# Moving the conditioning products of a two-block transformer between stages, and summing each of their steps in SBUF

## The chip, the cores and the metric

The kernel runs on one core of one Trainium2 chip. The metric is the device time of one execution, in microseconds (us). A core has five engines with queues of their own, each of which issues in order: TensorE (PE; its weight loads are shown apart as PEld), VectorE (DVE), ScalarE (ACT), GpSimd (POOL) and SyncE (SP), which issues DMAs; POOL issues DMAs too. TensorE's clock is granted in two levels, 1.2 and 2.4 GHz; a profile shows the granted level as a share of the full one.

## The reference

Two transformer blocks follow each other on 256 tokens of width 1024, all in float32. The first has two layers (a mixer, a feed-forward of 4096, a gated side input). The second has two layers with a second stream, the context, and its normalisations are shifted, scaled and gated by six rows of 1024 that a conditioning vector gives. This is the part that the change moves:

```python
for i in range(DEPTH):
    mod = (s_lat @ w_mod[i] + b_mod[i])[:, None, :]
    mod_c = s_ctx @ w_mod[i] + b_mod[i]
    sh1, sc1, g1, sh2, sc2, g2 = jnp.split(mod, 6, axis=-1)
    sh1c, sc1c, g1c, sh2c, sc2c, g2c = jnp.split(mod_c, 6, axis=-1)
    h = rms_norm_2(x, norm_mix[i]) * (1.0 + sc1) + sh1
    hc = rms_norm_2(xc, norm_mix[i]) * (1.0 + sc1c) + sh1c
    ...
    x = x + g1 * y
    h = rms_norm_2(x, norm_ffn[i]) * (1.0 + sc2) + sh2
    x = x + g2 * swiglu(h, w_gate[i], w_up[i], w_down[i])
```

`w_mod` is 2 x 1024 x 6144 floats. The products `s @ w_mod` depend on no token, so they can be computed anywhere ahead of their first use. Below, modulation (l, j) is the row j of layer l: 0 sh1, 1 sc1, 2 g1, 3 sh2, 4 sc2, 5 g2.

## The kernel before, in words

The main chain is four layers one after another: `block1_layer` twice (a mixer, its output projection, a layer norm, a feed-forward of eight groups, a second layer norm, a gated addition) and `block2_layer` twice (a mixer, its output projection, a normalisation, a feed-forward of eleven groups). A projection with float32 accuracy is three passes over the halves of a split: `wh` and `wl` are high and low part of a weight tile (ACT makes `wh` on line 214, DVE `wl` on line 216, from a tile that SP has loaded four units ahead), `xh` and `xl` those of the data. Beside the main chain runs other work that needs no result of it: the context stream, and the 12 modulations.

A modulation is four items of `part` (line 940, L952 its load, L954 its matmuls, L962 its addition). An item takes two k-steps. A k-step loads 128 rows of `w_mod` (512 KB) through a DMA that POOL issues into one of two buffers named `fr` (the first six into `bc`), and multiplies them with the conditioning vectors in four matmuls, one for each quarter of 256 columns, each in 32 columns of the array of its own. So there are 48 items and 96 k-steps in all. The four items of a modulation add up in one PSUM tile `fil`, of which there is one buffer, held from the first item to the last; then DVE adds the bias row (line 962) and, save for the gates, a matmul on line 968 turns the row.

Where an item stands is written in lists. `program` is a list of (weights needed, function); `weave` spreads one list through another, `side_by_side` puts the items of a second list between the pieces of a feed-forward. In the first layer, modulations (0,0), (0,1) and (0,2) are woven into the mixer (`mix`), (0,3) beside the first feed-forward group (`first`), and (0,4) stands at the layer's end (`last`). In the second, (0,5) and (1,0) are in the mixer, (1,1) in `first`, (1,2) in `last`. In the third there is none. In the fourth, (1,3), (1,4) and (1,5) are woven into the second half of the mixer and into the output projection (`swa`). A scheduler then orders the instructions of each engine by its own estimate of times, within about the place that the lists give.

Other things that POOL does in the same queue matter here: line 385 computes the power of a half for every normalisation (`stb`, from `sta` of DVE).

Of the kernel before, what the change touches and what calls it, by code (L numbers as in the profile page):

```python
# [10 lines left out]
F32 = mybir.dt.float32  # L11
# [3 lines left out]
ALU = mybir.AluOpType  # L15
# [104 lines left out]
def body(ctx: ExitStack, tc: tile.TileContext, A: dict, out: bass.AP):  # L120
# [817 lines left out]
    def modulation(l, box, js):  # L938
# [3 lines left out]
        def part(j, u):  # L942
# [3 lines left out]
            if u == 0:  # L946
                st[j] = PT("fil")
            ps = st[j]
            for k in (2 * u, 2 * u + 1):
                early[0] += 1  # L950
                raw = T([P, D], F32, "bc" if early[0] <= 6 else "fr", 2)
                nc.gpsimd.dma_start(raw, A["w_mod_2"][l, k * P:(k + 1) * P, j * D:(j + 1) * D])  # L952
                for g in range(4):
                    mm(ps[32 * g:32 * g + 32, 0:256], cT[:, k, :], raw[:, 256 * g:256 * g + 256],  # L954
                       start=(k == 0), stop=(k == KD - 1), tile_position=(0, 32 * g))
            if u < 3:
                return
            bm = T([P, 256], F32, "gate" if j in (2, 5) else "bm", 3 if j in (2, 5) else 1)
            V.memset(bm, 0.0)
            for s in range(2):  # L960
                nc.gpsimd.dma_start(bm[s:P:32, :], A["b_mod_2"][l, j * D:(j + 1) * D].rearrange("(g n) -> g n", g=4))
            V.tensor_tensor(bm, ps[:, 0:256], bm, ALU.add)  # L962
# [452 lines left out]
    def block2_layer(l, xT, pr, box, ce, done, side):  # L1415
# [30 lines left out]
        if l == 1:  # L1446
            rest = dense[:16] + weave(dense[16:] + g, side["swa"][:8])
            att = attention(e, pr, l, range(6), ce, y)
            prog += weave(rest, att[:-1], True) + [do(rows)] + weave(att[-1:], outp[:1])
            prog += weave([do(gla_out, e, y)] + outp[1:], side["swa"][8:-2]) + side["swa"][-2:]  # L1450
# [208 lines left out]
    def mod(l, *js):  # L1659
        return modulation(l, boxes[l], js)  # L1660

    program += block1_layer(0, xTs[0], to_next(1), dict(tail=flat(ctx_a[:1]), lr=4, mix=mod(0, 0, 1) + ctx_n + mod(0, 2), first=flat(ctx_a[1:2]) + mod(0, 3), ffn=ctx_a[2:-2],
                                                        end=flat(ctx_a[-2:]), last=mod(0, 4)))
    program += block1_layer(1, xTs[1], to_next(2), dict(tail=[], lr=6, mix=mod(0, 5) + mod(1, 0), first=mod(1, 1), ffn=ctx_b[:-2],
                                                        end=flat(ctx_b[-2:]), last=mod(1, 2)))
# [6 lines left out]
        "na": ffn_n, "swa": ffn_c, "pre": [], "from": 2, "ffn": [do(layer2_params, 1, prs[1])] + G(["norm", "kv", "znv", "gla"]), "end": L(["nk", "skv"])})  # L1672
    program += block2_layer(1, xTs[3], prs[1], boxes[1], ce1, to_next(4), {
        "swa": mod(1, 3, 4, 5), "from": 11, "ffn": [], "end": [],
# [51 lines left out]
```

## Time and profile before

| | us |
|---|---|
| three runs | 1934.02, 1938.44, 1940.81 |
| median | 1938.44 |
| the profiled execution | 1940.12 |
| its span, first to last instruction | 1938.3 |
| PE busy in it | 1862.2 (96%) |
| DVE, ACT, POOL busy | 1217.7, 984.7, 117.1 |

A row of a timeline gives the start in us, the duration, the engine, the line, the operation, what it writes and reads, the count of merged instructions, and in brackets how long the engine was idle before it and what ended that. One k-step is x8 there (four matmuls of two passes each).

### The profile page before, as it was taken

How to read it: one execution, taken by the hardware profiler on the slowest of the kernel's cores; microseconds unless marked ns; L12 is line 12 of the kernel's file. 1: busy time of each engine (PE TensorE's matmuls, PEld its weight loads, DVE VectorE, ACT ScalarE, POOL GpSimd, SP SyncE). 2: the span in 40 equal slices, each digit the busy share in tenths (PEclk: the TensorE clock that was granted, in tenths of full speed). 3: DMA queues.
4: the chain of work that ended last, by engine and by line, in shares of the span. 5: the costliest groups of instructions: out<-in, count | busy, mean ns of one | idle time of the engine just before them, and what ended most of it. 6: DMA issues, size and time to landing. Idle time of an engine off the chain costs nothing. (4 is left out here: it accounts for less than half of the span.)

```text
span 1938.3 us, 31903 instructions
## 1 busy us (share of the span) xinstructions
PE 1862.2 (96%) x12481; PEld 1586.0 (82%) x12481; DVE 1217.7 (63%) x2317; ACT 984.7 (51%) x1622; POOL 117.1 (6%) x194
## 2 busy tenths in 40 slices
PE   8989999999999999999899999999999999879997
PEld 6756798897887698887687899899999986659997
DVE  5564656656666656667576776685646776655555
ACT  6453455544555455553557664454556655334443
POOL 3111100000110100000000000000000001100000
PEclk9998999999999999999899999999999999989999
DMA  8744754545666654556453445556555455346563
GB/s 295 247 161 152 231 187 153 185 153 190 212 218 203 210 165 137 168 176 204 147 169 94 133 151 170 183 170 192 181 185 164 144 168 180 110 152 184 183 179 107
DMA packets 101411, 338.84 MB, mean 175 GB/s; under 512 B 12148, under 2 KB 13388, under 8 KB 101260
## 3 DMA queue, kind: packets, MB, share of 16 engines
q1 hardware_dynamic: 86124, 286.00, 46.3%
q0 software_dynamic: 15136, 50.80, 7.8%
q8 instruction: 98, 1.61, 0.3%
q14 instruction: 53, 0.43, 0.1%
HBM read 335.70 MB, written 1.05 MB: 174 GB/s over the span
## 5 line engine op out<-in xcount | busy, mean ns | idle before, releaser
L216 DVE TENSOR_TENSOR wl<-wr,wh 128x1024 fp32r<-128x1024 f32 (+3 forms) x562 | 638.1, 1137 | 400.2 <-ACT wh L214 397.0
L214 ACT CAST wh<-wr 128x1024 fp32r<-128x1024 f32 (+3 forms) x562 | 549.6, 980 | 639.5 <-PE acc L281 145.5
L279 PE MATMUL acc<-wh,mh 128*128 128x256 f32 (+3 forms) x400 | 132.0, 335 | 0.3 <-ACT mh L357 0.2
L280 PE MATMUL acc<-wl,mh 128*128 128x256 f32 (+3 forms) x400 | 130.8, 328 | 0.5 <-DVE wl L216 0.5
L281 PE MATMUL acc<-wh,ml 128*128 128x256 f32 (+3 forms) x400 | 130.6, 329 | 0.0
L279 PE MATMUL acc<-wh,xh 128*128 128x512 f32 (+3 forms) x304 | 117.9, 398 | 2.8 <-ACT xh L378 1.9
L280 PE MATMUL acc<-wl,xh 128*128 128x512 f32 (+3 forms) x304 | 119.8, 395 | 0.5 <-DVE wl L216 0.5
L281 PE MATMUL acc<-wh,xl 128*128 128x512 f32 (+3 forms) x304 | 117.7, 388 | 0.1
L850 PE MATMUL acc<-wh,a 128*128 128x512 f32 x256 | 101.5, 400 | 0.0
L852 PE MATMUL acc<-wh,a 128*128 128x512 f32 x256 | 101.1, 396 | 0.0
L851 PE MATMUL acc<-wl,a 128*128 128x512 f32 x256 | 101.0, 395 | 0.0
L1470 PE MATMUL sc<-xh,wh 128*128 128x256 f32 x352 | 100.6, 286 | 0.0
L1471 PE MATMUL sc<-xl,wh 128*128 128x256 f32 x352 | 100.3, 285 | 0.0
L1472 PE MATMUL sc<-xh,wl 128*128 128x256 f32 x352 | 100.2, 285 | 0.0
L1471 PE MATMUL sc<-ml,wh 128*128 128x256 f32 x352 | 98.8, 281 | 0.0
L1472 PE MATMUL sc<-mh,wl 128*128 128x256 f32 x352 | 98.7, 280 | 0.0
L1470 PE MATMUL sc<-mh,wh 128*128 128x256 f32 x352 | 98.6, 280 | 0.0
L954 PE MATMUL fil<-fr,cT 128*32 128x256 f32 x720 | 67.2, 419 | 28.1 <-DMA fr<-in_w_mod_dram 27.8
L952 POOL DMA_DIRECT2D fr<-in_w_mod_dram x90 | 48.5, 541 | 709.8 <-PE fil L954 581.7
L279 PEld LDWEIGHTS acc<-wh,mh 128*128 128x128 f32 x400 | 74.9, 189 | 14.1 <-issue 4.7
L280 PEld LDWEIGHTS acc<-wl,mh 128*128 128x128 f32 x400 | 75.3, 188 | 7.7 <-DVE wl L216 1.4
L281 PEld LDWEIGHTS acc<-wh,ml 128*128 128x128 f32 x400 | 75.1, 188 | 6.4 <-issue 0.6
(574 smaller groups left out, 4780.7 us busy)
## 6 DMA issues: line engine op xcount, KB each, us to landing
wr<-in_ffn_w_dram SPq DMA_DIRECT2D x128, 512.0 KB, 3.4
fr<-in_w_mod_dram POOLq DMA_DIRECT2D x90, 512.0 KB, 5.1
wr<-in_w_gate_dram SPq DMA_DIRECT2D x66, 512.0 KB, 3.7
wr<-in_w_up_dram SPq DMA_DIRECT2D x66, 512.0 KB, 4.3
wr<-in_w_down_dram SPq DMA_DIRECT2D x66, 512.0 KB, 4.0
wr<-in_w_in_dram SPq DMA_DIRECT2D x40, 384.0 KB, 3.3
wr<-in_ev_w_in_dram SPq DMA_DIRECT2D x28, 512.0 KB, 4.9
wr<-in_w_in_dram SPq DMA_DIRECT2D x28, 512.0 KB, 4.2
```

What stands on the lines that cost most here:

```text
L214: S.copy(hi, raw)
L216: V.tensor_tensor(lo, raw, hi, ALU.subtract)
L279: mm(o, xh[:, k, :], wh[:, kk, :], start=(u == 0 and kk == 0), stop=False)
L280: mm(o, xh[:, k, :], wl[:, kk, :], start=False, stop=False)
L281: mm(o, xl[:, k, :], wh[:, kk, :], start=False, stop=(u == nu - 1 and kk == 1))
L850: mm(o, hh[:, b, ts_], wh[:, kk, :], start=(b == 0), stop=False)
L851: mm(o, hh[:, b, ts_], wl[:, kk, :], start=False, stop=False)
L852: mm(o, hl[:, b, ts_], wh[:, kk, :], start=False, stop=(b == 3))
L954: mm(ps[32 * g:32 * g + 32, 0:256], cT[:, k, :], raw[:, 256 * g:256 * g + 256], start=(k == 0), stop=(k == KD - 1), tile_position=(0, 32 * g))
L1470: mm(o, wh[:, kk, bs], mh, start=(k == 0 and b == 0), stop=False, skip_group_check=True)
L1471: mm(o, wh[:, kk, bs], ml, start=False, stop=False, skip_group_check=True)
L1472: mm(o, wl[:, kk, bs], mh, start=False, stop=(k == 7), skip_group_check=True)
```

## The change

It does three things. An item now sums only its own two k-steps in PSUM and adds them to the row in SBUF, which is allocated, cleared and loaded with the bias at the first item; `fil` is free again after each item. Modulations (0,2), (0,3), (0,4), (1,1), (1,2) and (1,5) are put into the side lists of the four feed-forwards: (0,2) and (0,3) into the first, (0,4) and (1,1) into the second, (1,2) into the third, (1,5) into the fourth. In the last layer the remaining two, (1,3) and (1,4), stand in the second half of the mixer, and its output projection has none beside it.

```diff
@@ -944,22 +944,21 @@
                 box["mf"] = T([P, 6, 2, KD], F32, "mf", 2)
             mf = box["mf"]
             if u == 0:
-                st[j] = PT("fil")
-            ps = st[j]
+                bm = st[j] = T([P, 256], F32, "gate" if j in (2, 5) else "bm", 3 if j in (2, 5) else 1)
+                V.memset(bm, 0.0)
+                for s in range(2):
+                    nc.gpsimd.dma_start(bm[s:P:32, :], A["b_mod_2"][l, j * D:(j + 1) * D].rearrange("(g n) -> g n", g=4))
+            bm, ps = st[j], PT("fil")
             for k in (2 * u, 2 * u + 1):
                 early[0] += 1
                 raw = T([P, D], F32, "bc" if early[0] <= 6 else "fr", 2)
                 nc.gpsimd.dma_start(raw, A["w_mod_2"][l, k * P:(k + 1) * P, j * D:(j + 1) * D])
                 for g in range(4):
                     mm(ps[32 * g:32 * g + 32, 0:256], cT[:, k, :], raw[:, 256 * g:256 * g + 256],
-                       start=(k == 0), stop=(k == KD - 1), tile_position=(0, 32 * g))
+                       start=(k == 2 * u), stop=(k == 2 * u + 1), tile_position=(0, 32 * g))
+            V.tensor_tensor(bm, ps[:, 0:256], bm, ALU.add)
             if u < 3:
                 return
-            bm = T([P, 256], F32, "gate" if j in (2, 5) else "bm", 3 if j in (2, 5) else 1)
-            V.memset(bm, 0.0)
-            for s in range(2):
-                nc.gpsimd.dma_start(bm[s:P:32, :], A["b_mod_2"][l, j * D:(j + 1) * D].rearrange("(g n) -> g n", g=4))
-            V.tensor_tensor(bm, ps[:, 0:256], bm, ALU.add)
             if j in (2, 5):
                 box[j] = bm
             else:
@@ -1444,10 +1443,10 @@
         outp = proj(("w_out_2", l), 8, HALVES, tiles_of(y), urgent(evac), (1,), first=l)
         g = gla(e, pr, lambda: ce.fin, True)
         if l == 1:
-            rest = dense[:16] + weave(dense[16:] + g, side["swa"][:8])
+            rest = dense[:16] + weave(dense[16:] + g, side["swa"])
             att = attention(e, pr, l, range(6), ce, y)
             prog += weave(rest, att[:-1], True) + [do(rows)] + weave(att[-1:], outp[:1])
-            prog += weave([do(gla_out, e, y)] + outp[1:], side["swa"][8:-2]) + side["swa"][-2:]
+            prog += [do(gla_out, e, y)] + outp[1:]
         else:
             main = weave(attention(e, pr, l, range(3, 6), ce, y), g) + [do(gla_out, e, y), do(rows)] + outp
             prog += weave(main, side["swa"][:-6]) + side["swa"][-6:]
@@ -1659,19 +1658,19 @@
     def mod(l, *js):
         return modulation(l, boxes[l], js)
 
-    program += block1_layer(0, xTs[0], to_next(1), dict(tail=flat(ctx_a[:1]), lr=4, mix=mod(0, 0, 1) + ctx_n + mod(0, 2), first=flat(ctx_a[1:2]) + mod(0, 3), ffn=ctx_a[2:-2],
-                                                        end=flat(ctx_a[-2:]), last=mod(0, 4)))
-    program += block1_layer(1, xTs[1], to_next(2), dict(tail=[], lr=6, mix=mod(0, 5) + mod(1, 0), first=mod(1, 1), ffn=ctx_b[:-2],
-                                                        end=flat(ctx_b[-2:]), last=mod(1, 2)))
+    program += block1_layer(0, xTs[0], to_next(1), dict(tail=flat(ctx_a[:1]), lr=4, mix=mod(0, 0, 1) + ctx_n, first=flat(ctx_a[1:2]),
+                                                        ffn=weave(ctx_a[2:-2], mod(0, 2, 3)), end=flat(ctx_a[-2:]), last=[]))
+    program += block1_layer(1, xTs[1], to_next(2), dict(tail=[], lr=6, mix=mod(0, 5) + mod(1, 0), first=[],
+                                                        ffn=weave(ctx_b[:-2], mod(0, 4) + mod(1, 1)), end=flat(ctx_b[-2:]), last=[]))
     ce1 = Stream(1)
     cl = ctx_last(ce1, prs[1], boxes[1])
     L = lambda ns: flat([cl[n] for n in ns])
     G = lambda ns: [it for n in ns for it in ([cl[n]] if n[0] != "g" and n != "norm" else cl[n])]
     ffn_n, ffn_c = ctx_ffn(boxes[0])
     program += block2_layer(0, xTs[2], prs[0], boxes[0], ce, to_next(3), {
-        "na": ffn_n, "swa": ffn_c, "pre": [], "from": 2, "ffn": [do(layer2_params, 1, prs[1])] + G(["norm", "kv", "znv", "gla"]), "end": L(["nk", "skv"])})
+        "na": ffn_n, "swa": ffn_c, "pre": [], "from": 2, "ffn": weave([do(layer2_params, 1, prs[1])] + G(["norm", "kv", "znv", "gla"]), mod(1, 2)), "end": L(["nk", "skv"])})
     program += block2_layer(1, xTs[3], prs[1], boxes[1], ce1, to_next(4), {
-        "swa": mod(1, 3, 4, 5), "from": 11, "ffn": [], "end": [],
+        "swa": mod(1, 3, 4), "from": 2, "ffn": mod(1, 5), "end": [],
         "pre": [do(lambda: last.update(fn=bcast_row(A["final_norm_2"])))]})
     run(program)
```

The queue of POOL around the layer norm in front of the first feed-forward, before: `stb` is the power for token tile 0 and then tile 1, `fr` the loads of k-steps (those of (0,3), then of (0,4)).

```order
L952 DMA fr_1987<-in_w_mod_dram 128x1024
L952 DMA fr_1993<-in_w_mod_dram 128x1024
L952 DMA fr_1999<-in_w_mod_dram 128x1024
L385 TENSOR_TENSOR stb_1672<-sta_1670,mhalf_67 128x1
L952 DMA fr_4649<-in_w_mod_dram 128x1024
L952 DMA fr_4655<-in_w_mod_dram 128x1024
L385 TENSOR_TENSOR stb_1723<-sta_1721,mhalf_67 128x1
```

The same place now (`h4stb` and `cstb` are powers of the mixer's head norm and of the context's norm):

```order
L385 TENSOR_TENSOR h4stb_1364<-h4sta_1362,mhalf_67 128x4
L385 TENSOR_TENSOR cstb_1386<-csta_1384,mhalf_67 128x1
L955 DMA fr_2333<-in_w_mod_dram 128x1024
L385 TENSOR_TENSOR stb_1630<-sta_1628,mhalf_67 128x1
L385 TENSOR_TENSOR stb_1681<-sta_1679,mhalf_67 128x1
L955 DMA fr_2442<-in_w_mod_dram 128x1024
L955 DMA fr_2448<-in_w_mod_dram 128x1024
```

No load stands between the two powers any more, and the loads of the feed-forward's first pairs stand around them.

TensorE at the end of the last layer's output projection, before: `L281` is the projection's last matmul, `L177` are the transposes of token tile 0 (`sc_17324`, `sc_17336`) and tile 1, `L1470` begins the feed-forward.

```order
L281 MATMUL acc_17348<-wh_17234,c_3068_15852 128x512
L954 MATMUL fil_17219<-fr_17410,cT_72 32x256 x4
L954 MATMUL fil_17219<-fr_17416,cT_72 32x256 x4
L954 MATMUL fil_17219<-fr_17422,cT_72 32x256 x4
L177 MATMUL sc_17324<-ident_61,a_3402_17321 128x128 x4
L177 MATMUL sc_17336<-ident_61,a_3402_17321 128x128 x4
L954 MATMUL fil_17219<-fr_17428,cT_72 32x256 x4
L954 MATMUL fil_17219<-fr_17434,cT_72 32x256 x4
L177 MATMUL sc_17386<-ident_61,a_3412_17383 128x128 x4
L177 MATMUL sc_17398<-ident_61,a_3412_17383 128x128 x4
L954 MATMUL fil_17219<-fr_17440,cT_72 32x256 x4
L985 MATMUL fil_19201<-gate_17446,cst_220 128x256 x2
```

And now, up to the feed-forward's first matmul (which is on line 1469):

```order
L957 MATMUL fil_17930<-fr_17937,cT_72 32x256 x4
L177 MATMUL sc_17377<-ident_61,a_3432_17374 128x128 x4
L957 MATMUL fil_18274<-fr_18275,cT_72 32x256
L177 MATMUL sc_17389<-ident_61,a_3432_17374 128x128 x4
L957 MATMUL fil_18274<-fr_18275,cT_72 32x256 x3
L957 MATMUL fil_18274<-fr_18281,cT_72 32x256 x4
L957 MATMUL fil_18618<-fr_18619,cT_72 32x256 x4
L177 MATMUL sc_17439<-ident_61,a_3442_17436 128x128 x4
L177 MATMUL sc_17451<-ident_61,a_3442_17436 128x128 x4
L957 MATMUL fil_18618<-fr_18625,cT_72 32x256 x4
L957 MATMUL fil_18962<-fr_18963,cT_72 32x256 x4
L1469 MATMUL sc_17469<-xh_17197,wh_17317 128x256
```

All but the last k-step of (1,5) stand ahead of the feed-forward, as before, although the list puts them into it. With two `fr` buffers, `fr_18275` can be loaded only after the pair ahead of it was used, `fr_18619` only after `fr_18275`, and `fr_18963` only after `fr_18619`.

TensorE in the first feed-forward before, between two weight tiles of an up part (`L825` to `L827` are its three passes):

```order
L825 MATMUL sc_2429<-xh_1607,wh_2384 128x256
L826 MATMUL sc_2429<-xl_1608,wh_2384 128x256
L827 MATMUL sc_2429<-xh_1607,wl_2386 128x256
L825 MATMUL sc_2428<-xh_1607,wh_2390 128x256
L826 MATMUL sc_2428<-xl_1608,wh_2390 128x256
L827 MATMUL sc_2428<-xh_1607,wl_2392 128x256
```

And in the same feed-forward now, where an item of (0,2) has been put:

```order
L825 MATMUL sc_2347<-xh_1565,wh_2284 128x256
L826 MATMUL sc_2347<-xl_1566,wh_2284 128x256
L827 MATMUL sc_2347<-xh_1565,wl_2286 128x256
L957 MATMUL fil_2441<-fr_2442,cT_72 32x256 x4
L957 MATMUL fil_2441<-fr_2448,cT_72 32x256 x4
L825 MATMUL sc_2346<-xh_1565,wh_2290 128x256
L826 MATMUL sc_2346<-xl_1566,wh_2290 128x256
```

In the feed-forwards the two k-steps of an item mostly stand together like this, with the next item some 100 to 350 matmuls further on. In the second layer's mixer, where (0,5) and (1,0) stand, the order of before is thinned out: 8 items where 16 were between the first layer's end and the second feed-forward.

## Rows read from the trace of the kernel before

**Rows 1.** The page: busy time by engine, and the granted clock in 40 slices.

```profile
PE 1862.2 (96%) x12481; PEld 1586.0 (82%) x12481; DVE 1217.7 (63%) x2317; ACT 984.7 (51%) x1622; POOL 117.1 (6%) x194
PEclk9998999999999999999899999999999999989999
```

**Rows 2.** Waits: who waited for whom, us in total, times, longest.

```profile
POOL fr L952 <- PE fil L954: 581.7, 56, 200.0
...
PE fil L954 <- DMA fr<-in_w_mod_dram: 27.8, 12, 7.4
```

**Rows 3.** Stretches: length, busy us and counts by engine, granted clock, DMA share, GB/s.

```profile
140.00:165.00 25.00, 19.16 (x112) 13.20 (x111) 7.48 (x27) 3.44 (x13) 2.11 (x4) 0.59 0.47 160
207.70:226.15 18.45, 15.93 (x82) 11.52 (x80) 14.22 (x24) 5.95 (x9) 3.44 (x7) 0.91 0.93 316
618.00:633.00 15.00, 11.00 (x53) 5.84 (x52) 5.01 (x26) 3.35 (x12) 1.85 (x4) 0.66 0.44 151
661.00:677.20 16.20, 12.27 (x66) 7.74 (x64) 14.85 (x32) 9.60 (x20) 6.21 (x9) 0.86 0.82 284
940.00:960.00 20.00, 12.20 (x61) 9.30 (x62) 9.48 (x22) 8.30 (x18) 1.93 (x4) 0.73 0.45 155
1715.50:1736.60 21.10, 9.92 (x70) 5.60 (x69) 9.91 (x22) 9.43 (x19) 3.60 (x6) 0.70 0.52 176
1400.00:1500.00 100.00, 100.00 (x664) 91.09 (x664) 53.92 (x66) 55.95 (x64) 0.00 (x0) 1.00 0.57 173
```

**Rows 4.** The page's groups: busy us, mean ns of one, idle before.

```profile
L954 PE MATMUL fil<-fr,cT 128*32 128x256 f32 x720 | 67.2, 419 | 28.1 <-DMA fr<-in_w_mod_dram 27.8
```

**Rows 5.** Timeline, TensorE, end of the first mixer.

```profile
145.22 1.08 PE L954 MATMUL fil<-fr,cT 128*32 128x256 f32 x8 [4.54 <-DMA fr<-in_w_mod_dram]
...
164.96 0.50 PE L279 MATMUL acc<-wh,mh 128*128 128x512 f32 x1
```

**Rows 6.** Timeline, layer norm in front of the first feed-forward.

```profile
214.40 0.15 DVE L383 TENSOR_SCALAR sta<-ag 128x1 f32<-128x1 f32 x1
218.39 0.53 POOL L952 DMA_DIRECT2D fr<-in_w_mod_dram  x1 [2.31 <-PE fil L954]
218.94 0.58 POOL L385 TENSOR_TENSOR stb<-sta,mhalf 128x1 f32<-128x1 f32 x1
226.15 0.28 PE L825 MATMUL sc<-xh,wh 128*128 128x256 f32 x1
```

**Rows 7.** Timeline, second layer: its attention, then the layer norm behind it.

```profile
622.41 1.08 PE L954 MATMUL fil<-fr,cT 128*32 128x256 f32 x8 [4.00 <-DMA fr<-in_w_mod_dram]
...
668.33 0.14 DVE L383 TENSOR_SCALAR sta<-ag 128x1 f32<-128x1 f32 x1
...
670.34 1.43 POOL L385 TENSOR_TENSOR stb<-sta,mhalf 128x1 f32<-128x1 f32 x1
```

**Rows 8.** Timeline, end of the second layer.

```profile
949.83 0.43 DVE L962 TENSOR_TENSOR gate<-fil,gate 128x256 f32<-128x256 f32 x1 [2.54 <-PE fil L954]
...
950.77 0.15 DVE L412 TENSOR_TENSOR ms<-ms 128x1 f32<-128x1 f32 x1
```

**Rows 9.** Timeline, end of the last output projection.

```profile
1715.50 1.07 PE L954 MATMUL fil<-fr,cT 128*32 128x256 f32 x16
1716.47 1.05 POOL L952 DMA_DIRECT2D fr<-in_w_mod_dram  x2 [13.52 <-PE fil L954]
1724.01 1.08 PE L954 MATMUL fil<-fr,cT 128*32 128x256 f32 x8 [7.44 <-DMA fr<-in_w_mod_dram]
1729.58 0.64 PE L954 MATMUL fil<-fr,cT 128*32 128x256 f32 x8 [1.87 <-DMA fr<-in_w_mod_dram]
1736.56 0.78 PE L1470 MATMUL sc<-xh,wh 128*128 128x256 f32 x1
```

**Rows 10.** The load's line (us) and the addition's line (ns): min/median/max.

```profile
DMA to landing us min/median/max: 3.9/5.2/12.8
...
L962 DVE TENSOR_TENSOR gate<-fil,gate x4: 424/425/426, 170.8 to 1734.6; 128x256 f32<-128x256 f32 x4
```

## The prediction, on record before the changed kernel was run

> **What bounds the kernel now.** I read the page first: TensorE is busy for 96% of the span and its clock is granted in full in most slices, at 0.8 or 0.9 in a few [rows 1]. So the end is set by TensorE, and time can come only from where it idles or runs at 1.2 GHz. Next the waits: the largest single wait of PE is that of a modulation's matmul for its load, 27.8 us in 12 places, and on the other side POOL waits 581.7 us for such matmuls, because a load may start only when one of two `fr` buffers is free [rows 2]. Then the stretches around these places [rows 3]. In a feed-forward (1400 to 1500) PE is busy throughout at full clock; whatever is put there is paid in full. The other six stretches, 116.4 us in all, are where it idles. Length less PE's busy time is what was idle, and (1 - clock) times the length is what the clock can have cost at most:
> 140-165: 5.8 and 10.3; 207.7-226: 2.5 and 1.7; 618-633: 4.0 and 5.1; 661-677: 3.9 and 2.3; 940-960: 7.8 and 5.4; 1715-1737: 11.2 and 6.3 [rows 3]. Together 66 us: the most that this change could touch. All six are chains (head products, a layer norm, a normalisation) in which PE has little else to do, and in all six modulations stand.
>
> Last I followed each stretch in the timeline, because two causes are mixed there: PE itself waits for a load, and POOL, which issues in order, holds the power that a normalisation needs behind a load that waits for PE.
>
> **The change part by part.**
>
> *Matmuls out and in.* By the order, five modulations leave the mixers and layer ends for the first three feed-forwards: 20 items, 40 k-steps. (1,5) does not: all but one of its k-steps still stand ahead of the fourth feed-forward. Before, a k-step costs 67.2 / 90 = 0.75 us (four matmuls to a k-step, 720 recorded) [rows 4], so 40 take 30 us; about ten of them lie inside a chain that ends no earlier for their going, so 22.4 us leave the path. They come back as 20 pairs at 1.07 us (as the first pair of [rows 9]), 21.4 us, in stretches at 100%. Sum +1.0. If all 40 were on the path it is +8.5, if twenty were hidden -6.5.
>
> *First mixer's end.* The 4.54 us wait goes with (0,2); the projection is reached at 164.96 [rows 5]. The clock of 0.59 there [rows 3] cost at most 10.3 us. What follows the wait is a chain of narrow matmuls, so I count 4 of it: sum 8.5. Bounds: 0 if the chain only shows its own waits in the place of this one, 14.8 if the clock stays up.
>
> *Layer norm in front of the first feed-forward.* DVE has the variance of tile 1 at 214.55, POOL starts the power at 218.94, behind a load that had to wait for PE [rows 6]: 4.4 us. In the new order no load stands between the two powers. What becomes late next is PE's own filler, projection work that is still owed, so I take 3 (0 to 4.4).
>
> *Second layer's attention.* The 4.00 us wait [rows 7] and the clock (at most 5.1 [rows 3], I take 3) go with (1,1). But the new order has the same narrow place once more, the last item of (1,0) only 19 matmuls behind its predecessor; I charge 2.5 for that. Sum 4.5 (0 to 9.1).
>
> *Layer norm behind it.* The variance of tile 1 is there at 668.47, the power starts at 670.34 and takes 1.43 instead of the 0.58 of the other place [rows 6, 7]: 1.9 + 0.85, of which I take 2.5 (0 to 2.7).
>
> *End of the second layer.* DVE stands 2.54 us before the gate's addition, which waits for the last k-step of (1,2), and the sum of squares of tile 1 queues behind it [rows 8]. Both go; with a little clock 3 (0 to 6).
>
> *End of the last output projection.* Here I expect a loss. Before, two loads are issued at 1716.47, PE waits 7.44, then a round of 1.87, and the feed-forward starts at 1736.56, 20.0 us behind the end of the first pair (1715.50 + 1.07) [rows 9]. In the new order three rounds of loads follow each other ((5,1), (5,2), (5,3), each needing a buffer that the one before frees), with the transposes between. With the first landing 7.5 us after its issue as before, and each later one 4 to 5 us after its own (between the smallest, 3.9, and the median, 5.2 [rows 10]), I get 8 + 1 + 1 + 4.5 + 1 + 4.5 + 1 = 21 from there, and the gate row's matmuls, now in the feed-forward, come on top with one. Sum -2. Bounds: +3 if the loads land at the smallest time, -9 if they all need 7.5.
>
> *Additions.* 36 more additions of 0.42 us [rows 10] are 15 us of DVE, which is busy 54 us in 100 in a feed-forward [rows 3]: nothing, unless one holds up a weight tile. SP loads a weight tile four units ahead, so DVE has that much room to split it. The cost if that cover fails is under 15. The row's clearing and bias move earlier and are on no path: nothing.
>
> By the rule of the Trainium skill (DMA: Bandwidth & Descriptors, Anatomy of one DMA, SWDGE path) a load from POOL takes about 2.0 us plus its bytes over 436 GB/s, an estimate of 3.2 us for 512 KB. The trace does not agree; its median is 5.2 [rows 10]. By the page the three rounds would be some 3 us shorter and this place worth +1.
>
> Sum: 1.0 + 8.5 + 3 + 4.5 + 2.5 + 3 - 2 = 20.5 us. From the profiled execution, 1940.1, that gives 1919.6. That execution (its span is 1938.3) was 1.7 above the median of the runs, 1938.4, so I put the median after at 1918. The bounds of the terms add up to -15 and +49.
>
> **The rivals.**
>
> *Moved work is paid and nothing is returned (slower).* The modulations were filler. In the six stretches the chains of DVE and ACT decide, PE's wait is only shown at the load, and every stretch keeps its length; then 21.4 us are added and only the k-steps outside the stretches are saved. These are some 20, 15 us, so +6.4, with 2 for the last projection: 1947. For it: DVE is busy 14.9 of 16.2 us at 661-677 [rows 3]. Against it: POOL's and DVE's rows show the chain itself held by loads and additions [rows 6 to 8]. It decides if the stretches together get less than 6 us shorter.
>
> *Everything comes back.* Without these waits PE keeps the full clock: 14.8, 4.4, 9.1, 2.7, 6 and matmuls at 8.5: 1938.4 - 45 = 1893; with the last projection as I count it 1895. Against it: chains remain, and one of the stretches with least wait, 661-677, is still at 0.86 [rows 3].
>
> *The last layer takes it back.* The change does not do what its list says for (1,5). With three rounds at 7.5 us the feed-forward starts 9 later there, and the same happens at the narrow place of (1,0), 5 us: 1918 + 7 + 3 = 1928, still faster.
>
> *One bank for every pair (about no change).* Each pair is a group of its own in the single `fil` buffer, and the next user of `fil` waits for an addition that stands in DVE's queue behind weight tiles. Estimated at two additions, 2 x 0.43 = 0.9 us [rows 10], at each of 20 pairs it is 17 us, and the gain is nearly spent: 1918 + 17 = 1935. Against it: in the feed-forwards at least 20 matmuls lie between a pair and the next user of `fil`. The Trainium skill (Perfetto Trace Analysis, Matmuls) says that independent groups should rotate through PSUM banks, so that an evacuation overlaps the next group; that speaks for this rival, and no row of before shows such a wait in a feed-forward.
>
> **How the numbers follow.** Forecast with its own spread (1905 to 1929) 0.57, last layer 0.15, everything 0.06, one bank 0.13, slower 0.09. A measurement of this kernel can tell about 0.3%, 5.8 us, from no change: faster is below 1932.6, slower above 1944.3. The first three cases are faster, one bank is half within and half faster, and the slower case and the last layer's reach a little into the middle: faster 0.82, same 0.11, slower 0.07. The range to hold 8 in 10: 1902 to 1936.
>
> **What would show it.** PE's wait for these loads falls from 27.8 to about 15, nearly all of it behind the last mixer's start. The stretch behind the first mixer is granted more than 0.59; no power of a layer norm starts more than 1 us behind its variance; the feed-forwards keep PE at 100% with pairs of 1.1 us; the last feed-forward starts 20 to 24 us behind the last projection matmul. I am wrong if the first feed-forward starts less than 15 us earlier than at 226.15, if PE waits for `fil` in a feed-forward, or if DVE waits for pairs while PE waits for weights.

## The result, and the profile after

The changed kernel takes 1953.64 us (median of 5 runs, 1947.89 to 1954.35) against 1938.44 before: a ratio of 1.0079 with the interval 1.0060 to 1.0097. It is slower by 15 us; the forecast was 1918, with a range of 1902 to 1936. The profiled execution has a span of 1952.2 us, against 1938.3 [rows 1].

The page of the changed kernel, busy times and granted clock:

```profile
PE 1866.5 (96%) x12481; PEld 1591.8 (82%) x12481; DVE 1229.1 (63%) x2353; ACT 985.5 (50%) x1623; POOL 117.8 (6%) x194
PEclk9998899999999899999899999999999999989999
```

PE is busy 4.3 us longer than in [rows 1] with the same count of matmuls, and idle 85.7 us instead of 76.1, so the page alone says little. The waits for the loads did what was forecast (11.3 us instead of 27.8 [rows 2]; 15 was forecast):

```profile
POOL fr L955 <- PE fil L957: 725.3, 51, 59.6
...
PE fil L957 <- DMA fr<-in_w_mod_dram: 11.3, 5, 3.8
```

The stretches that answer to [rows 3] (the same columns; they are cut at the same matmuls of the main chain, so their times have moved), and 100 us of a feed-forward:

```profile
129.00:144.25 15.25, 11.07 (x90) 8.82 (x87) 11.59 (x37) 9.04 (x24) 1.16 (x2) 1.00 0.38 121
192.30:210.20 17.90, 13.04 (x50) 9.65 (x48) 13.56 (x23) 5.48 (x8) 2.52 (x2) 0.81 0.60 197
624.40:631.70 7.30, 6.93 (x45) 4.67 (x44) 5.99 (x32) 4.45 (x17) 1.20 (x2) 1.00 0.61 212
656.50:676.00 19.50, 11.15 (x47) 8.00 (x45) 17.61 (x35) 9.84 (x21) 2.91 (x4) 0.79 0.59 209
948.30:965.00 16.70, 10.18 (x44) 8.54 (x45) 9.71 (x24) 9.31 (x21) 1.08 (x2) 0.79 0.16 47
1728.70:1750.50 21.80, 10.71 (x67) 4.63 (x66) 11.61 (x25) 9.28 (x19) 5.57 (x8) 0.67 0.60 202
1400.00:1500.00 100.00, 100.00 (x673) 89.88 (x673) 52.84 (x63) 54.89 (x63) 2.11 (x4) 1.00 0.62 198
```

Together 98.5 us instead of 116.4. The first mixer's end went from 25.0 to 15.3 and keeps the full clock; the second layer's attention from 15.0 to 7.3; the layer norm behind that got longer, 19.5 instead of 16.2. So these places gave time back, and the loss is elsewhere. It is seen when the spans of the first three feed-forwards are set beside each other, each from its first matmul to its last. Before:

```profile
226.15:452.89 226.74, 226.74 (x1526) 205.12 (x1525) 140.43 (x188) 119.72 (x161) 4.04 (x6) 1.00 0.51 164
677.22:887.89 210.67, 210.67 (x1366) 181.00 (x1367) 136.19 (x230) 110.72 (x190) 0.60 (x1) 0.99 0.51 165
1302.30:1520.91 218.61, 218.61 (x1509) 201.65 (x1508) 131.47 (x165) 115.41 (x144) 1.10 (x2) 1.00 0.56 172
sum 656.02, PE 656.02 PEld 587.77 DVE 408.10 ACT 345.85 POOL 5.74; mean PE 218.67 PEld 195.92 DVE 136.03 ACT 115.28 POOL 1.91
```

And the changed kernel:

```profile
210.16:455.96 245.80, 244.03 (x1669) 212.97 (x1670) 143.88 (x199) 120.31 (x163) 13.78 (x24) 0.99 0.56 187
675.97:901.76 225.79, 225.79 (x1483) 188.10 (x1484) 138.65 (x241) 109.96 (x189) 9.78 (x18) 0.99 0.55 187
1307.66:1535.45 227.79, 225.90 (x1569) 205.73 (x1568) 130.91 (x166) 117.10 (x145) 4.34 (x8) 1.00 0.58 184
sum 699.38, PE 695.72 PEld 606.81 DVE 413.44 ACT 347.36 POOL 27.90; mean PE 231.91 PEld 202.27 DVE 137.81 ACT 115.79 POOL 9.30
```

The three feed-forwards grew by 43.4 us, and the forecast had put 21.4 there. Everything outside them is 29.5 us shorter (1938.3 - 656.0 less 1952.2 - 699.4), where the forecast had 41.9. A single pair costs what was forecast. TensorE, first feed-forward after the change:

```profile
278.32 0.28 PE L827 MATMUL sc<-xh,wl 128*128 128x256 f32 x1
278.53 1.07 PE L957 MATMUL fil<-fr,cT 128*32 128x256 f32 x16
279.54 0.39 PE L825 MATMUL sc<-xh,wh 128*128 128x256 f32 x1
```

Without the pair the next matmul would start 0.12 us after 278.32; it starts 1.22 after, so the pair took 1.10. Twenty of them are 22 us; another 21 us in the feed-forwards were not foreseen.

### The profile page after: what moved, and what is told of

It reads as the page before. It is cut to its first block, busy times and chain, and to the rows that moved or that the text cites. A ratio compares the mean times of both kernels' runs of the same rounds, so it can differ in the third digit from the quotient of the medians.

```text
span 1952.2 us, 31983 instructions
## 1 busy us (share of the span) xinstructions
PE 1866.5 (96%) x12481; PEld 1591.8 (82%) x12481; DVE 1229.1 (63%) x2353; ACT 985.5 (50%) x1623; POOL 117.8 (6%) x194
## 4 chain that ended last, share of the span: by engine, by line
PE 57%; issue 3%; DVE 3%; ACT 1%; DMA 1%; POOL 0%; POOLq 0%; ACTq 0%; DVEq 0%
PE sc L1469 4%; PE sc L1470 4%; PE sc L1471 4%; PE acc L279 3%; PE acc L280 3%; PE acc L281 3%; PE acc L1495 2%; PE acc L1496 2%; PE acc L1497 2%; PE sc L825 2%; PE sc L827 2%; PE sc L826 2%; PE acc L850 2%; PE acc L852 2%; PE acc L851 2%
## 5 line engine op out<-in xcount | busy, mean ns | idle before, releaser
L281 PE MATMUL acc<-wh,ml 128*128 128x256 f32 (+3 forms) x400 | 133.1, 335 | 0.0
L281 PE MATMUL acc<-wh,xl 128*128 128x512 f32 (+3 forms) x304 | 116.7, 385 | 0.1
L1469 PE MATMUL sc<-mh,wh 128*128 128x256 f32 x352 | 99.8, 284 | 1.9 <-ACT t L1475 1.9
L1470 PE MATMUL sc<-ml,wh 128*128 128x256 f32 x352 | 100.1, 284 | 0.0
L1470 PE MATMUL sc<-xl,wh 128*128 128x256 f32 x352 | 99.9, 284 | 0.0
L281 PEld LDWEIGHTS acc<-wh,ml 128*128 128x128 f32 x400 | 77.1, 193 | 7.3 <-issue 0.5
L825 PE MATMUL sc<-mh,wh 128*128 128x256 f32 x256 | 75.4, 296 | 2.4 <-DVE ml L358 2.4
```

What stands on the lines that cost most here:

```text
L281: mm(o, xl[:, k, :], wh[:, kk, :], start=False, stop=(u == nu - 1 and kk == 1))
L825: mm(o, wh[:, kk, bs], mh, start=(k == 0 and b % 2 == 0), stop=False, skip_group_check=True)
L1469: mm(o, wh[:, kk, bs], mh, start=(k == 0 and b == 0), stop=False, skip_group_check=True)
L1470: mm(o, wh[:, kk, bs], ml, start=False, stop=False, skip_group_check=True)
```

## The experiments

All times are medians of the runs that are compared, and a ratio is to the kernel before on the same chip, with its 95% interval. The experiments were timed in four sets, in which the kernel before took 1934.0 to 1938.5 us. So a difference of two medians from different sets is uncertain by some us, and where it matters the same difference by the two ratios, in us, stands beside it.

### The parts one at a time

**The summing alone** (`sum_only`): the edit of `part`, every list as before.

```diff
-                st[j] = PT("fil")
-            ps = st[j]
+                bm = st[j] = T([P, 256], F32, "gate" if j in (2, 5) else "bm", ...)
+            bm, ps = st[j], PT("fil")
...
+            V.tensor_tensor(bm, ps[:, 0:256], bm, ALU.add)
```

> Only the summing in SBUF, every modulation where it stood before. Theory A (what is put into a feed-forward is paid in full, and it disturbs the context work there): no placement is changed, so 1938 +- 4 us, feed-forwards as long as before. Theory B (the 36 more additions and the shared fil buffer hold up chains wherever a modulation stands): most of the 15 us that the change cost shows here, 1948 to 1953 us.

1922.82 us, ratio 0.9933 (0.9912 to 0.9955). Neither theory had it: the edit that the forecast priced at nothing is the one that gains, 13.5 us. The feed-forwards are unchanged to 0.8 us, as they should be, since hardly any modulation stands in them here; what the 36 more additions cost elsewhere is less than what comes back:

```profile
sum 655.28, PE 655.28 PEld 587.01 DVE 408.21 ACT 345.98 POOL 5.74; mean PE 218.43 PEld 195.67 DVE 136.07 ACT 115.33 POOL 1.91
```

**Each move alone, with the summing** (`ff1`, `ff2`, `ff3`, `ff4`: one feed-forward's list as in the change, the others as before). For the first:

```diff
...
-mix=mod(0, 0, 1) + ctx_n + mod(0, 2), first=flat(ctx_a[1:2]) + mod(0, 3), ffn=ctx_a[2:-2],
+mix=mod(0, 0, 1) + ctx_n, first=flat(ctx_a[1:2]), ffn=weave(ctx_a[2:-2], mod(0, 2, 3)),
...
```

> SBUF summing, and of the moves only (0,2) and (0,3) into the first feed-forward. Theory A: the traces of before and after differ by -16 us up to the start of the first feed-forward and +17 in it, so about 1940 us. Theory B: as the run with the summing alone, about 1950 us. A third view, that the moves as a whole gain what was forecast in the mixer and only later feed-forwards lose it: 1925 us.

> SBUF summing, and of the moves only (0,4) and (1,1) into the second feed-forward. Theory A: -4 us between the first and second feed-forward, +15 in the second, so about 1949 us, the worst of the parts. Theory B: as the run with the summing alone.

> SBUF summing, and only the last layer's change: (1,3) and (1,4) in the second half of its mixer, (1,5) listed in its feed-forward. Theory A: -5 us in mixer and output projection, +1.4 in the feed-forward: about 1935 us. Theory B: as the run with the summing alone. The forecast of before the result (three rounds of loads at the end of the output projection): 1940 us or more.

> SBUF summing, and of the moves only (1,2) into the third feed-forward. Theory C (the summing alone gains 13.5 us, every move then costs more than it gives back): if the parts add up, 30.8 us between the changed kernel and the summing alone, less 9.7, 3.8 and 6.8 for the other three moves, leave 10.5 for this one, 1933 us. Rival (only the four pairs at 1.09 us and two stalls of 2 us in that feed-forward, less 7 us at the end of the second layer): 1925 us.

In this order, `ff1`, `ff2`, `ff4` and `ff3`: 1932.50 (0.9985, 0.9970 to 0.9999), 1926.59 (0.9950, 0.9930 to 0.9970), 1929.60 (0.9956, 0.9940 to 0.9972) and 1933.55 (0.9972, 0.9956 to 0.9987). Against the summing alone the moves cost 9.7, 3.8, 6.8 and, for (1,2), 10.7 us (7.6 by the ratios, as it is of another set). That is 31.0 together, and the changed kernel is 30.8 slower than the summing alone; by the ratios it is 25 and 28. So the parts add up within the noise. Theory A's numbers for single moves, taken from the two traces, were off by up to 22 us, 13.5 of it because they took the summing for nothing; the second feed-forward's move, expected to be the worst, is the cheapest.

**The moves without the summing** (`place_only`):

> The four moves, with a modulation summed in PSUM as before. Theory D: the context work in the feed-forwards, which uses fil as well, has to go around whole modulations: slower than the changed kernel, 1957 us or more. Rival (the 36 additions on DVE cost time in the feed-forwards): faster than the changed kernel, below 1950 us.

2012.07, ratio 1.0377 (1.0351 to 1.0403). Its three feed-forwards take 764.6 us, 108.6 more than before. With a modulation held in `fil` from its first item to its last, other users of that one buffer can't come between. In the trace at least the last four k-steps of each of the five modulations run one behind the other, and PE waits for their loads. These are PE's waits for loads in the three feed-forwards (us, times, longest):

```profile
PE fil L954 <- DMA fr<-in_w_mod_dram: 15.4, 7, 4.9
...
PE fil L954 <- DMA fr<-in_w_mod_dram: 15.3, 5, 6.1
...
PE fil L954 <- DMA fr<-in_w_mod_dram: 6.4, 4, 2.9
```

That is 37 us; in the changed kernel PE waits for none there. The granted clock is 0.92 to 0.96 in these feed-forwards, where the changed kernel has 0.99. So the summing is what makes the moves bearable at all, and the rival, that the additions are the burden, falls.

### Why the summing gains

**`hold`**: the summing, but one `fil` tile for the four items of a modulation.

```diff
-            bm, ps = st[j], PT("fil")
+            if u == 0:
+                st[j, "ps"] = PT("fil")
+            bm, ps = st[j], st[j, "ps"]
```

> SBUF summing with the old placement, but the four items of a modulation share one fil tile, which is so held from the first item to the last, as before the change. Theory D (the summing gains because fil is free between items): the gain goes, 1934 to 1940 us. Rival (it gains because the row is cleared and its bias loaded at the first item, off the end of the modulation): 1921 to 1926 us.

1924.76 (0.9923, 0.9903 to 0.9943): the gain stays, so theory D, that the gain comes from `fil` being free between items, falls.

**`bias_early`**: the kernel before, with only the clearing and the bias load at the first item.

> The kernel before, in which only the clearing of the row and the loading of its bias are moved from a modulation's last item to its first; the items add up in PSUM as before. Theory F (the summing in SBUF gains because the bias loads no longer stand in POOL's queue at the modulation's end): 1921 to 1926 us. Rival (the gain comes from where the order puts the k-steps once each item is a group of its own): 1936 to 1940 us.

1936.36 (1.0004, 0.9990 to 1.0017): no gain, so theory F falls too. What both runs that gain (`sum_only`, `hold`) have in common, and neither the kernel before nor `bias_early` has, is that each item is a group that ends with an addition. PE's waits for the loads, 27.8 us before [rows 2], are 22.0 in `hold`, 26.3 in `bias_early` and, in `sum_only`, 18.1 (in total, times, longest):

```profile
PE fil L957 <- DMA fr<-in_w_mod_dram: 18.1, 11, 4.4
```

About half of the gain stands in the last layer: from the third feed-forward's start to the fourth's it is 434.3 us before, 427.2 in `sum_only`, 427.4 in `hold` and 433.0 in `bias_early`. At the end of that stretch the difference is one of order. The end of the last output projection, TensorE, in the run with the summing alone:

```profile
1700.64 1.07 PE L957 MATMUL fil<-fr,cT 128*32 128x256 f32 x16
1704.41 1.52 PE L177 MATMUL sc<-ident,a 128*128 128x128 f32 x8 [2.69 <-DVE a L996]
1708.80 1.08 PE L957 MATMUL fil<-fr,cT 128*32 128x256 f32 x8 [2.86 <-DMA fr<-in_w_mod_dram]
1710.87 1.08 PE L957 MATMUL fil<-fr,cT 128*32 128x256 f32 x8 [0.99 <-DMA fr<-in_w_mod_dram]
...
1718.30 0.50 PE L1469 MATMUL sc<-xh,wh 128*128 128x256 f32 x1
```

Before, the k-step that waits 7.44 us for its load stands ahead of the transposes of token tile 0 [rows 9]; here the transposes come first, and the wait is 2.86. From the first pair's start to the feed-forward it is 17.7 us instead of 21.1. The k-step in question in `hold`, where it stands behind the transposes too, and in `bias_early`, where it stands ahead of them as before:

```profile
1713.42 1.08 PE L959 MATMUL fil<-fr,cT 128*32 128x256 f32 x8 [2.89 <-DMA fr<-in_w_mod_dram]
```

```profile
1720.17 1.08 PE L958 MATMUL fil<-fr,cT 128*32 128x256 f32 x8 [6.05 <-DMA fr<-in_w_mod_dram]
```

So the order goes with the gain in all four kernels. It shows 3.4 us of the 7.1 between the two feed-forwards; the rest stands ahead of that end, and which waits went there was not followed. That the addition, for which the next item must wait, is what makes the scheduler put the transposes first is argued and not shown: a version that ends each item's group without an addition was not run.

**`spread`**: the summing, and the last two items of (1,5) spread through the output projection instead of behind it.

```diff
-            prog += weave([do(gla_out, e, y)] + outp[1:], side["swa"][8:-2]) + side["swa"][-2:]
+            prog += weave([do(gla_out, e, y)] + outp[1:], side["swa"][8:])
```

> SBUF summing with the old placement, but the last two items of (1,5) no longer stand behind the output projection of the last layer; all four are spread through it. Theory C (in a dense stretch a pair costs 1.09 us, at the projection's end PE waits for the loads): the end is some 5 us shorter and the projection 2.2 us longer, 1920 us. Rival (the end is the chain of the normalisation, and the pairs are hidden in it): 1925 us.

1920.57 (0.9902, 0.9882 to 0.9922), 2.2 us less than the summing alone (6.0 by the ratios), about what was expected from paying 2.2 for two pairs and getting some 5 back. In the traces it is 424.7 us from the third feed-forward's start to the fourth's, 2.5 less. The difference is not clear of the noise.

### Why the feed-forwards grew by more than the pairs

**An address** (`after_al`). In the three kernels with the first feed-forward's move (the changed one, `ff1`, `place_only`) the matmuls of the second and third feed-forward followed each other at a median of 119 to 121 ns, in all others at 117. What they had in common was where the tile `mh`, the data operand of these matmuls, stood in SBUF: the first use of small tiles had moved ahead of it.

```diff
     def new_xT(tag, new=None, kd=KD):
+        if tag == "m" and "pad" not in csts:
+            csts["pad"] = T([P, 48], F32, "pad")
+            V.memset(csts["pad"], 0.0)
```

> The changed kernel, with 192 unused bytes in front of the tile mh, so that mh stands at 185088 in SBUF (256 bytes past a multiple of 512, as in the kernel before) instead of 184896 (64 past one). In all kernels run so far the matmuls of the second and third feed-forward start 117 ns apart (median) where mh stands at 184576 and 119 to 121 ns where it stands at 184896, whatever else differs. Theory E (the address of the streamed operand sets this step): back to 117 ns, 7 us less, 1946 to 1948 us. Rival (the loads moved into the first feed-forward, or chance): 119 to 121 ns again and 1953 us.

1945.27 (1.0042, 1.0026 to 1.0057), 8.4 us less than the changed kernel (7.2 by the ratios), with the step back at 117 ns. Eleven us inside one block of 96 up matmuls of the third feed-forward, the changed kernel and then this run (after the length: PE's busy time, with the count of matmuls in brackets):

```profile
1338.00:1349.00 11.00, 11.00 (x94) 11.00 (x93) 5.91 (x5) 4.69 (x5) 0.00 (x0) 1.00 0.58 186
```

```profile
1326.80:1337.80 11.00, 11.00 (x96) 11.00 (x95) 5.96 (x5) 4.71 (x5) 0.00 (x0) 1.00 0.65 187
```

Worked out from the 96 starts the step is 120.0 ns there and 116.7 here. PE counts as busy throughout in both, at full clock: only the count shows it. In `ff1`, which puts nothing into the second and third feed-forward, these two are 5.3 us longer than with the summing alone, so over half of the 9.7 us of that move is the address.

**The pairs taken away** (`empty`) and **the lists left in place** (`bundle`), both with `mh` at its good address:

```diff
...
-ffn=weave(ctx_a[2:-2], mod(0, 2, 3))
+ffn=bundle(ctx_a[2:-2], mod(0, 2, 3))   # an item is run with an entry of the context's list
...
```

> The changed kernel with mh back at its good address (1945 us), without the loads, matmuls and additions of the 20 items that stand in the first three feed-forwards; their rows, bias loads and turning matmuls remain, and the items keep their places in the lists. Theory G (only the pairs themselves are paid, 20 by 1.09 us): 1945 less 22 is 1923 us. Rival (the pairs also hold up the context work of the feed-forwards, by loads, by the fil buffer or by order): some 10 us more go, 1913 us. Second rival (the lists themselves, woven together, have moved the context work to worse places): the feed-forwards stay longer than in the run with the summing alone by more than the turning matmuls, 1930 us.

> The changed kernel with mh at its good address, but the items are bound to entries of the context's list instead of being entries of their own, so that the context work keeps the places that it had in the feed-forwards before. Second rival of the run before: the waits of the context work in the feed-forwards go, 1937 us or less. Theory G: 1945 us as without it.

`empty`: 1917.48 (0.9910, 0.9891 to 0.9929), 27.8 us less than `after_al` (25.6 by the ratios), where the pairs alone would be 22. `bundle`: 1933.89 (0.9998, 0.9987 to 1.0008), 11.4 us less (8.5 by the ratios) with all pairs still run: the second rival is right. `side_by_side` counts entries; when eight more stand in the list, the context work moves to other places. The three feed-forwards together in `after_al`, `bundle` and `empty`:

```profile
sum 693.89, PE 690.24 PEld 601.31 DVE 413.53 ACT 347.30 POOL 27.80; mean PE 230.08 PEld 200.44 DVE 137.84 ACT 115.77 POOL 9.27
```

```profile
sum 686.25, PE 685.84 PEld 600.54 DVE 413.96 ACT 346.68 POOL 27.81; mean PE 228.61 PEld 200.18 DVE 137.99 ACT 115.56 POOL 9.27
```

```profile
sum 664.09, PE 661.30 PEld 592.62 DVE 406.84 ACT 347.06 POOL 8.62; mean PE 220.44 PEld 197.54 DVE 135.61 ACT 115.69 POOL 2.87
```

The pairs are 29.8 of it (693.9 - 664.1), 1.5 us each: 1.1 on PE and 0.4 of what they hold up. Without any pair the three are still 8.8 us longer than with the lists of before (655.3). Binding the items to the context's entries gives back 7.6 (693.9 - 686.3). The waits that come with the new places are these in the changed kernel, and `bundle` has neither:

```profile
372.27 0.71 PE L1113 MATMUL acc<-t,t 64*128 64x128 f32 x4 [0.85 <-DVE t L1106]
...
1393.01 0.39 PE L1469 MATMUL sc<-mh,wh 128*128 128x256 f32 x1 [1.89 <-ACT t L1475]
```

The rest of the 7.6 shows as no wait of 0.7 us or more, and was not followed further.

### The version that the runs point to

No move pays, the summing does, and addresses are free. `best_x` is `spread` with `xh` moved by 32 bytes and `mh` by 256; in `best_w` the weight tiles move too; in `best3` they stay, and `a4` and `c4` are moved.

Of the edit of `best3`, with remarks added:

```diff
+            csts[tag] = T([P, 8], F32, "pad" + tag)     # 32 bytes ahead of xh, and of mh
...
+            csts["c4"] = T([P, 24], F32, "padc")        # best3: 96 bytes ahead of c4, and of a4
```

> The run with the summing and the spread items, with 32 unused bytes in front of xh and 224 behind the tiles after it: xh stands at 82944 (a multiple of 512) instead of 82912, mh at another multiple of 512, the weight tiles where they were. Theory E: the matmuls of the first and fourth feed-forward, 120 ns apart in every kernel so far, go to 117: 1800 of them by 3 ns, 5 us less than the spread run, 1915 us. Rival: 120 ns and 1920 us.

> The same, with the 32 bytes in front of the weight tiles, so that wr, wh and wl start at multiples of 512 too (before: 32 short of one). Theory E, if it holds for every streamed operand: the projections and the down halves of the feed-forwards stream weight tiles of 512 columns, 232 to 236 ns apart; with 3 ns less on each of some 4500 of them another 13 us less, 1902 us. If only xh and mh matter: as the run without this, 1915 us.

> The run with the summing, the spread items and xh moved (1915 us), with two more paddings, so that a4 and c4 stand at the same distance from a multiple of 128 bytes as the weight tiles (96), and xh and mh at another (0). Theory H (a step of two matmuls depends on whether the two operands stand at the same distance: equal is good where 512 columns are streamed, 228 against 233 ns, and bad where 256 are, 120 against 117): the down halves (1345 recorded steps by 5 ns) and the steps with c4 (297 by 4 ns) get faster, 8 us, 1907 us. Rival (only the streamed operand's own address counts): 1915 us.

1915.07 (0.9886, 0.9868 to 0.9904), 1918.37 (0.9902, 0.9882 to 0.9922) and 1905.90 (0.9853, 0.9839 to 0.9868). The last is 28 us faster than the kernel before on the same chip, and beats both kernels. Its page:

```profile
PE 1835.9 (96%) x12481; PEld 1568.0 (82%) x12481; DVE 1227.5 (64%) x2357; ACT 984.0 (52%) x1622; POOL 118.0 (6%) x194
```

For `best_x` theory E had the time, but not what it is made of: 3071 recorded steps of `xh` with 256 columns became 2.9 ns shorter (8.8 us), as forecast, and 928 steps of `xh` and `c4` with 512 columns 4.3 ns longer (4.0 us), which it had not. For `best_w` it failed: the steps with 512 columns fell to 228 ns, but those with 256 stood at 120, in all four feed-forwards. Theory H forecast `best3` to about a microsecond; its term for `a4` came (7.2 us), that for `c4` did not. The count of matmuls in 11 us of the fourth feed-forward, up part, in `spread`, `best_x` and `best_w`:

```profile
1747.30:1758.30 11.00, 11.00 (x94) 11.00 (x93) 6.04 (x5) 4.74 (x6) 0.00 (x0) 1.00 0.61 185
```

```profile
1746.10:1757.10 11.00, 11.00 (x96) 11.00 (x95) 6.03 (x5) 4.79 (x6) 0.00 (x0) 1.00 0.60 193
```

```profile
1744.20:1755.20 11.00, 11.00 (x94) 11.00 (x93) 6.04 (x5) 4.85 (x6) 0.00 (x0) 1.00 0.65 193
```

## Why the prediction was wrong, point by point

**Matmuls out and in: the step that failed.** It was priced at +1.0: 22.4 us out, 21.4 in. In the feed-forwards 43.4 came in. Of that are 22 for the pairs, as forecast; 5.5 for the address of `mh` (699.4 - 693.9); 7.6 for the context's places (693.9 - 686.3); the remaining 8 are mostly the pairs' hold-ups (29.8 - 22), and a few matmuls of the context and of the rows' turning (143 more matmuls in the first feed-forward, of which 128 are pairs). The premise was right, that whatever is put into a stretch at 100% is paid in full. What failed was to take the pairs for all that is put there. The lists decide where everything else in them stands, and the order of allocation decides addresses; both were there to be read ahead of the run, though not what an address costs. This is 22 us of the miss. The other 12 are time that did not come back outside the feed-forwards (29.5 us instead of 41.9), and even of the 29.5 only 11 to 16 us belong to the moves: the rest comes with the summing alone (the range is from the profiled executions, 1252.8 against 1263.7 us outside, to the ratios).

**Additions: nothing.** Right in the feed-forwards, where PE waits for no weight tile after the change, and wrong as a whole. The edit was judged by what it adds to DVE. What it does to the order gains 13.5 us, the largest single term, and the forecast credited all gain to the moves. The sum's sign came from there: with the summing at -13.5 the moves are at +31.

**First mixer's end, and the layer norm behind it.** The mechanisms were right, the first gain was half of what it seemed. The wait goes and the clock stays up (1.00 instead of 0.59), 9.8 us. But what follows, up to the layer norm, is 5.4 us longer and has the lower clock instead, since its own chain now comes without filler: PE has 169 recorded matmuls there instead of 216, and idles 7.5 us. Before and after:

```profile
165.00:207.70 42.70, 42.70 (x216) 30.01 (x217) 25.54 (x35) 20.80 (x44) 7.42 (x11) 1.00 0.60 190
```

```profile
144.25:192.30 48.05, 40.60 (x169) 32.34 (x170) 27.74 (x41) 25.67 (x55) 4.21 (x5) 0.89 0.37 118
```

Behind it no load stands between the powers:

```profile
198.73 0.14 DVE L383 TENSOR_SCALAR sta<-ag 128x1 f32<-128x1 f32 x1
198.96 0.98 POOL L385 TENSOR_TENSOR stb<-sta,mhalf 128x1 f32<-128x1 f32 x1 [1.04 <-DVE sta L383]
...
210.16 0.38 PE L825 MATMUL sc<-xh,wh 128*128 128x256 f32 x1 [2.12 <-DVE xl L358]
```

The first feed-forward starts 16.0 us earlier than in [rows 6], a little above the mark that was set. But part of that the summing alone returns: its feed-forward starts at 220.97, and in `ff2`, `ff3`, `ff4` and `spread`, which have the summing and the same lists ahead of it, at 219.7 to 225.4. The layer norm's stretch itself is 0.6 us shorter, where 3 was forecast, and what PE waits for last is now DVE's `xl`.

**Second layer's attention, and the layer norm behind it.** The attention's stretch got 7.7 us shorter, within the bounds. The norm's got 3.3 longer, where 2.5 less was forecast, which is the slower rival's mechanism at one place. DVE, POOL and PE there:

```profile
663.76 0.15 DVE L383 TENSOR_SCALAR sta<-ag 128x1 f32<-128x1 f32 x1
664.06 0.92 POOL L385 TENSOR_TENSOR stb<-sta,mhalf 128x1 f32<-128x1 f32 x1 [0.45 <-DVE sta L383]
...
671.57 1.97 PE L177 MATMUL sc<-ident,x 128*128 128x128 f32 x8 [3.77 <-DVE ml L358]
...
672.83 2.48 DVE L911 SCALAR_TENSOR_TENSOR a<-a,plb,bc 128x1024 f32<-128x1024 f32 x2 [0.59 <-POOL plb L385]
...
675.97 0.58 PE L825 MATMUL sc<-mh,wh 128*128 128x256 f32 x1 [2.42 <-DVE ml L358]
```

The power starts 0.15 us behind the end of its variance, as it should, and PE waits for DVE anyway, 3.77 and 2.42 us, with no filler left. DVE is busy 17.6 of the 19.5 us. The row that said so was quoted in the forecast (14.9 of 16.2 us), but only in favour of the slower rival; the term for this norm did not use it. From the end of the first feed-forward to the second it is 4.3 us less (224.3 to 220.0), where some 16 were forecast: 7 for the two chains and 9 for the sixteen k-steps that left (22.4 / 40 each).

**End of the second layer.** From the second feed-forward to the third it is 8.5 us less (414.4 to 405.9), where 3 for the chain and 4.5 for eight k-steps were forecast. That it comes out is partly luck: with the summing alone it is 411.0, so 3.5 of the 8.5 belong to a term that was put at nothing.

**End of the last output projection.** Right as a place, -0.7 instead of -2. TensorE, after:

```profile
1736.35 1.03 PE L957 MATMUL fil<-fr,cT 128*32 128x256 f32 x2 [2.76 <-DMA fr<-in_w_mod_dram]
1743.89 1.08 PE L957 MATMUL fil<-fr,cT 128*32 128x256 f32 x8 [3.83 <-DMA fr<-in_w_mod_dram]
...
1749.51 1.08 PE L957 MATMUL fil<-fr,cT 128*32 128x256 f32 x8 [1.63 <-DMA fr<-in_w_mod_dram]
```

There are three rounds of loads as forecast, in 21.8 us instead of 21.1 [rows 3]. Against the summing alone, where this end takes 17.7 us, the whole move in the last layer costs 6.8 us.

**The rivals.** "Moved work is paid and nothing is returned" had the sign and 1947, for another reason: it was to decide if the stretches got less than 6 us shorter, and they got 17.9 shorter. "One bank" did not happen: the pairs in the feed-forwards cost 1.1 us on PE and none waits for `fil` there. The rule of the Trainium skill that was weighed for it (Perfetto Trace Analysis, Matmuls: independent groups should rotate through different PSUM banks) has no price here for groups of two k-steps, and no run with a second `fil` buffer shows what rotating would give. Holding the one buffer for all eight k-steps of a modulation does cost, +74 us in the moves without the summing, where PE waits for loads.

## What to carry to other kernels

Filler that stands in an idle stretch costs less there than its own time, and in a full one it costs its own time and what it displaces: here the moves gave back 11 to 16 us and cost 43 where the work was put. So before filler is moved, ask which stretches at 100% receive it, and follow every other entry of the list that it is put into. An edit that only seems to make a move possible should be run by itself: here it was the only part that gained. And where busy time, clock and order agree and a stretch is still longer, compare counts of instructions in equal windows, and addresses.

## What the runs showed of the hardware

How fast matmuls follow each other depends on where the two operands stand in SBUF, by 2 to 3%, and PE counts as busy all the while. Mean step, in feed-forwards and projections, by the offset from a multiple of 128 bytes of the weight tiles and of the other operand (`xh`, `mh`, `a4` or `c4`), from the starts of all such matmuls of a run:

| weights, other | 256 columns | 512 columns | seen in |
|---|---|---|---|
| 96, 96 | 119.8 ns | 228 to 229 ns | `spread` (`xh`), `best3` (`a4`) |
| 0, 0 | 119.8 ns | 228 ns | `best_w` |
| 96, 0 | 116.8 ns | 233 ns | `best_x`, `best3` (`xh`, `mh`) |
| 96, 64 | 119.9 ns | 234 ns | the changed kernel (`mh`) |

Equal offsets are good where 512 columns are streamed and bad where 256 are; the fourth row is slow in both, so equality alone is not the rule. `c4` in `best3` is equal by this count and yet went from 228.9 ns in `spread` to 232.6. Counted from a multiple of 256 bytes it is not equal: it starts at 99424, 96 past one, and `wh` at 50144, 224 past one, as `a4` at 138464. By that count the steps with 512 columns of all these runs agree, 228 to 229 ns where both operands are equal and 233 to 234 where they aren't; this was found afterwards and no run tests it. The mechanism stays open. What can be used is the number: 256 bytes of padding are worth some 12 us of this kernel (`spread` to `best3`: the recorded steps add up to 12.2, the medians, of different sets, differ by 14.7 and the ratios by 9.5).
